# Two decay tiles for the S5 scan, gates' outputs in the input pool, other shares of matmuls between the parameters' steps

## The chip, the cores and the metric

One core of one Trainium2 chip runs the whole program in one launch. The metric is the time of an execution on the device in microseconds, as a median of several runs: 2692.31 us before the change (three runs, 2691.86 to 2693.35). The names of engines in the profile: PE is TensorE's matmuls and PEld its weight loads, DVE is VectorE, ACT is ScalarE, POOL is GpSimd, SP is the engine whose queue (SPq) issues the DMAs.

## The reference, cut to what matters

One encoder layer on x of 2048 tokens by 1024, float32:

```python
proj = rmsnorm(x, norm1_g) @ w_in
q, k, v, u, g_attn, g_ssm = split(proj)
attn = windowed_gqa(rope(q), rope(k), v, sink)          # |i-j| <= 128
ssm = bidirectional_s5(u, lam, log_dt, b, c, d, w_glu)  # 32 groups x 16 channels, 64 states, two directions
merged = sigmoid(g_attn) * (attn @ w_attn_branch) + sigmoid(g_ssm) * (ssm @ w_ssm_branch)
x = x + merged @ w_out
x = x + (silu(h2 @ w_ffn_gate) * (h2 @ w_ffn_up)) @ w_ffn_down   # h2 = rmsnorm(x)
y = rmsnorm(x)
```

In S5 each direction has the state recurrence h[t] = exp(lam dt) h[t-1] + Bbar u[t], and the output is Re(C (h_fwd + h_bwd)) + d u, then GELU and a gated linear unit.

## The kernel before, in words

Matmul operands are split into a high and a low float32r part and multiplied in three passes. All weights come through one pool of raw tiles, ScalarE or GpSimd writes the high part (lines 413, 415) and VectorE the low part (line 416). The gates' 32 column blocks (function `gates`) are matmuls at line 450: 48 for one block of 128 columns and one half of the tokens, evicted from the PSUM tag pj (two banks) by ScalarE's tanh at line 588 into a tile `go`, which a DMA stores to DRAM (gD). They depend on little, and serve as filling between other work.

The S5 parameters (`ssm_prep`) are computed in the first phase, under projections and gates of the first half of tokens. First come 32 tables of angles (tiles wt from products wn on GpSimd and wv on VectorE, lines 232 to 234, stored to cD), a yield after each fourth; then for eight batches of four groups the matrices E and F (tiles ef, products wm, same lines, on VectorE), a small tile bk (GpSimd: a memset at line 309, two copies at line 312, two buffers), a yield, and `ssm_turn`: TensorE transposes E (line 326) and multiplies bk with F (line 332), ScalarE and VectorE read the result (lines 334 to 341), DMAs store it (eD, tD). ef has four buffers, that is two batches. `ssm_prep` is a generator, and what it yields is a number of us: phase 1 then issues so many us of the main stream (a step of three matmuls at line 450 counts 0.681), and at the end the rest of it. TensorE's order there is the order of the program, written by hand. The other engines' order is fixed at build by a planner, which simulates the program and takes instructions by order of program, operands and free buffers.

Attention and the second half's projections follow, and then phase 2, the S5 scan over 16 pairs of groups (`ssm_pair`), again with TensorE's order by hand: for each pair X, 4.3 us of gates of the second half, the output matmuls (lines 398 to 400) of the pair two before, 4.3 us of gates. A pair runs so: TensorE makes X in PSUM (line 360), VectorE four products m with the angle tables (lines 365 to 368), GpSimd adds them to Y (lines 371, 372), ScalarE writes the decay tile A (line 376, two copies), VectorE runs the two scans, forward on one half of the partitions and backward on the other (lines 382, 383), reading A and Y and writing W; then four products n, in tiles of the same tag m (lines 385, 386, 388 on GpSimd, 387 on VectorE), their sums H (line 390 on GpSimd, 391 on VectorE), later TensorE's output matmuls and the GELU (lines 402 and 404 on ScalarE, 403 and 405 on VectorE). Behind this comes `branch_a_quarter`, attention's branch matmuls with operands `at`.

The input pool (`act`, tag a) has 20 tiles of 4 KB a partition; 16 hold the normalised input h of the second half in phase 2. In the scan's own pool m has six tiles, Y and W two, A one, and go two. What the change and the prediction touch: lines 248, 313, 364, 370, 384, 808.

Of the kernel before, what the change touches and what calls it, by code (L numbers as in the profile page):

```python
# [40 lines left out]
G0 = 3  # L41
# [24 lines left out]
def run(gen, us):  # L66

    while us > 0:
        c = next(gen, None)
        if c is None:  # L70
            break
        us -= c
    return us
# [13 lines left out]
def rest(gen):  # L87
    for _ in gen:
        pass


class Kern:
# [58 lines left out]
    def ssm_prep(self, pool, lam_re, lam_im, log_dt, b_re, b_im, c_re, c_im, d):  # L151
# [7 lines left out]
        W = lambda sh: pool.tile(sh, F32, tag="w", name="w")  # L159
# [70 lines left out]
        def outer(eng, fr, tag, a0, a1, op, dst, sh):  # L230
            m1, m2 = (fr.tile(sh, F32, tag=tag, name=tag) for _ in range(2))
            eng.tensor_tensor(m1, a0[0], a0[1], MULT)
            eng.tensor_tensor(m2, a1[0], a1[1], MULT)
            eng.tensor_tensor(dst, m1, m2, op)

        with ExitStack() as es:
            sub = self.pool("prept", 3, es)
            cc, cs = angles(sub, 17, 32, "t")
            sh2 = [128, 16, 16]
            lo = lambda z, g: z[:, g, 0:16].unsqueeze(1).to_broadcast(sh2)  # L240
            hi = lambda z, g: z[:, g, 16:32].unsqueeze(2).to_broadcast(sh2)
            for g in range(G):
                T = sub.tile([128, 2, 16, 16], F32, tag="wt", name="wt")
                e, tg = (p, "wn") if g % 2 == 0 else (v, "wv")
                outer(e, sub, tg, (lo(cc, g), hi(cc, g)), (lo(cs, g), hi(cs, g)), SUB, T[:, 0], sh2)
                outer(e, sub, tg, (lo(cc, g), hi(cs, g)), (lo(cs, g), hi(cc, g)), ADD, T[:, 1], sh2)
                if g % 4 == 3:
                    yield 14.5
                self.store(self.cD[:, g], T.rearrange("q r a b -> q r (a b)"))

        ce, se = angles(pool, 0, 17, "e")
# [44 lines left out]
        sh = [128, NG, 8, CH]  # L296
# [4 lines left out]
        for g0 in range(0, G, NG):  # L301
            E, F = (sub.tile([128, NG, 2, 8, CH], F32, tag="ef", name="ef", bufs=4) for _ in range(2))
            outer(v, sub, "wm", (ab(ewr, g0, 0), bb_(B[:, 0], g0)), (ab(ewi, g0, 0), bb_(B[:, 1], g0)), SUB, E[:, :, 0], sh)
            outer(v, sub, "wm", (ab(ewr, g0, 0), bb_(B[:, 1], g0)), (ab(ewi, g0, 0), bb_(B[:, 0], g0)), ADD, E[:, :, 1], sh)
            outer(v, sub, "wm", (ab(ce, g0, 8), bb_(C[:, 0], g0)), (ab(se, g0, 8), bb_(C[:, 1], g0)), SUB, F[:, :, 0], sh)
            outer(v, sub, "wm", (ab(ce, g0, 8), bb_(C[:, 1], g0)), (ab(se, g0, 8), bb_(C[:, 0], g0)), ADD, F[:, :, 1], sh)
            self.store(self.fD[:, g0:g0 + NG], F.rearrange("q g r t h -> q g r (t h)"))
            bk = sub.tile([128, 2, NG, 48], F32, tag="bk", name="bk", bufs=2)
            p.memset(bk, 0.0)
            for dd in range(2):  # L310
                q = slice(64 * dd, 64 * dd + 64)
                p.tensor_scalar(bk[q, :, :, 32 * dd:32 * dd + 16], bb[q, :, g0:g0 + NG], 1.0, 1.0, MULT, MULT)
            yield 8.5
            self.ssm_turn(pool, g0, NG, E, F, bk, dd_)
        es.close()

# [29 lines left out]
    def ssm_pair(self, pool, g0):  # L346

        nc, v, s, p, pe = self.nc, self.v, self.s, self.p, self.pe
        tl = lambda tag, sh, bufs: pool.tile(sh, F32, tag=tag, name=tag, bufs=bufs)
        E, U, cs = tl("E", [128, 2, 2, 128], 2), tl("U", [128, 2, NC], 4), tl("cs", [128, 2, 2, NC], 2)  # L350
        self.load(E, self.eD[:, g0:g0 + 2])
        for i in range(2):
            f0 = CH * (g0 + i)
            self.load(U[:, i], self.uD[:, f0:f0 + CH, :])
        self.load(cs, self.cD[:, g0:g0 + 2])
        X = []
        for r in range(2):
            x = self.ps("a" if r == 0 else "b", [128, 2, NC])
            for i in range(2):
                pe.matmul(x[:, i], E[:, i, r], U[:, i], start=True, stop=True)  # L360
            X.append(x)
        co, si = cs[:, :, 0], cs[:, :, 1]
        sh = [128, 2, NC]
        m = [tl("m", sh, 6) for _ in range(4)]
        v.tensor_tensor(m[0], X[0], co, MULT)
        v.tensor_tensor(m[1], X[1], si, MULT)
        v.tensor_tensor(m[2], X[1], co, MULT)
        v.tensor_tensor(m[3], X[0], si, MULT)
        sh2 = [128, 2, 2, NC]
        Y, W, a = tl("Y", sh2, 2), tl("W", sh2, 2), tl("A", sh2, 1)  # L370
        p.tensor_tensor(Y[:, 0], m[0], m[1], ADD)
        p.tensor_tensor(Y[:, 1], m[3], m[2], SUB)
        p.memset(Y[0:64, :, :, NC - 1:NC], 0.0)
        p.memset(Y[64:128, :, :, 0:1], 0.0)
        for i in range(2):
            s.activation(a[:, :, i], self.edge.unsqueeze(1).to_broadcast([128, 2, NC]), AF.Copy,
                         scale=self.r8[:, g0 + i:g0 + i + 1])
        Wf, Yf, af = (z.rearrange("q r g c -> q (r g c)") for z in (W, Y, a))
        n = 4 * NC
        p.memset(Wf[0:64, 0:1], 0.0)  # L380
        p.memset(Wf[64:128, n - 1:n], 0.0)
        v.tensor_tensor_scan(Wf[0:64, 1:n], af[0:64, 0:n - 1], Yf[0:64, 0:n - 1], 0.0, MULT, ADD)
        v.tensor_tensor_scan(Wf[64:128, n - 2::-1], af[64:128, n - 1:0:-1], Yf[64:128, n - 1:0:-1], 0.0, MULT, ADD)
        n = [tl("m", sh, 6) for _ in range(4)]
        p.tensor_tensor(n[0], W[:, 0], co, MULT)
        p.tensor_tensor(n[1], W[:, 1], si, MULT)
        v.tensor_tensor(n[2], W[:, 0], si, MULT)
        p.tensor_tensor(n[3], W[:, 1], co, MULT)
        H = [tl("H", sh, 4) for _ in range(2)]
        p.tensor_tensor(H[0], n[0], n[1], ADD)  # L390
        v.tensor_tensor(H[1], n[3], n[2], SUB)
        F, T = tl("F", [128, 2, 2, 128], 2), tl("T", [128, 2, 128], 2)
        self.load(F, self.fD[:, g0:g0 + 2])
        self.load(T, self.tD[:, g0:g0 + 2])
        yield
        y = self.ps("nt" if g0 % 4 else "c", sh)
        for i in range(2):
            pe.matmul(y[:, i], T[:, i], U[:, i], start=True, stop=False)
            pe.matmul(y[:, i], F[:, i, 0], H[0][:, i], start=False, stop=False)
            pe.matmul(y[:, i], F[:, i, 1], H[1][:, i], start=False, stop=True)  # L400
        g = tl("g", sh, 2)
        s.activation(g, y, AF.Square, scale=math.sqrt(0.044715))
        v.scalar_tensor_tensor(g, g, 1.0, y, ADD, MULT)
        s.activation(g, g, AF.Tanh, scale=0.7978845608028654)
        v.scalar_tensor_tensor(g, g, 1.0, y, ADD, MULT)
        for i in range(2):
            f0 = CH * (g0 + i)
            self.store(self.yD[f0:f0 + CH].rearrange("h t c -> t h c"), g[:, i])
# [387 lines left out]
    def phase2(self, w_in, w_ab):  # L796
        self.yD = self.dram.tile([512, L, NC], F32, name="yD")
        self.ma = {}
        self.mid_es = ExitStack()
        self.mid = self.pool("mid", 1, self.mid_es)  # L800
        self.hi_on_act = True
        with ExitStack() as es:
            pool = self.pool("p2", 1, es)
            self.edge = pool.tile([128, NC], F32, name="edge")
            self.p.memset(self.edge, 1.0)
            self.p.memset(self.edge[0:64, NC - 1:NC], 0.0)
            self.p.memset(self.edge[64:128, 0:1], 0.0)
            gt = self.gates(w_in, self.H1, 1, G0, 16, 1, pool, bufs=2)
            with self.tc.manual_schedule(engines={mybir.EngineType.PE}):
                due = run(gt, 15.0)  # L810
                P = [self.ssm_pair(pool, g) for g in range(0, G, 2)]
                for i in range(len(P) + 2):
                    if i < len(P):
                        next(P[i])
                    due = run(gt, due + 4.3)
                    if i > 1:
                        rest(P[i - 2])
                    due = run(gt, due + 4.3)
                rest(gt)
        W = self.branch_a_weights(w_ab)  # L820
        for q in range(4):
            self.branch_a_quarter(W, q)
# [460 lines left out]
```

## Time and profile before

| what | value |
|---|---|
| median of three runs | 2692.31 us |
| profiled execution, its own time | 2696.69 us |
| its span | 2694.9 us |
| mean granted TensorE clock | 0.978 |
| TensorE busy | 2566.2 us, 95% |
| VectorE busy | 1899.0 us, 70% |
| GpSimd busy | 1237.3 us, 46% |
| ScalarE busy | 1033.9 us, 38% |

The span runs from the first to the last instruction, the execution's own time also holds what lies around it. Busy shares are means over stages that differ; a row of the waits or of the timeline gives an engine's idle time before an instruction and, behind an arrow, what ended it. The granted clock is a share of 2.4 GHz, and 0.5 is 1.2 GHz.

### The profile page before, as it was taken

Reading aid. Unit: us, or ns where it says so; the run is one execution under the profiler, and the core shown is the slowest. Engines: PE = TensorE matmul, PEld = TensorE weight load, DVE = VectorE, ACT = ScalarE, POOL = GpSimd, SP = SyncE. Lnnn points to the kernel's source line nnn. Section 1 sums busy time; section 2 is a strip of 40 time slices with the busy share of each in tenths; the row PEclk is TensorE's granted clock in tenths of the full one; section 3 lists DMA queues with packets and bytes.
Section 4 is the critical chain, followed back from the end, with each engine's and each line's share of the span. In section 5 each row is a group of like instructions: output and inputs, shape, how many; then the busy total and the mean of one; then the engine's idle time right before and its main releaser. Section 6 shows DMA issues by size and latency. Waiting matters only on the chain.

```text
span 2694.9 us, 34635 instructions
## 1 busy us (share of the span) xinstructions
PE 2566.2 (95%) x12090; PEld 2124.8 (79%) x12090; DVE 1899.0 (70%) x2734; ACT 1033.9 (38%) x1878; POOL 1237.3 (46%) x1007
## 2 busy tenths in 40 slices
PE   8997999999999899999979999998999999999998
PEld 7886889988777678887758888877888887877887
DVE  5889477776677847656568888877777776466567
ACT  4222265676222213443454444444444445111113
POOL 2387122222455502215227667746656663354336
PEclk9998999999999899999989999999999999999999
DMA  5345542333554456666566565656455557676547
GB/s 163 105 142 196 162 151 77 93 83 107 179 165 150 144 138 197 199 201 211 190 203 184 172 180 156 187 178 202 141 155 145 161 150 240 253 282 238 222 181 261
DMA packets 451918, 467.95 MB, mean 174 GB/s; under 512 B 82848, under 2 KB 381856, under 8 KB 446624
## 3 DMA queue, kind: packets, MB, share of 16 engines
q1 hardware_dynamic: 451744, 465.75, 54.9%
q8 instruction: 95, 1.56, 0.2%
q14 instruction: 79, 0.65, 0.1%
HBM read 299.99 MB, written 165.68 MB: 173 GB/s over the span
## 4 chain that ended last, share of the span: by engine, by line
PE 42%; DVE 5%; DMA 3%; POOL 2%; issue 2%; ACT 1%; POOLq 0%; DVEq 0%; ACTq 0%; SPq 0%
PE ps_b L1003 17%; PE ps_pj L1003 11%; PE ps_a L1003 11%; DVE w L956 2%; PE ps_a L900 1%; PE ps_pj L450 1%; PE ps_b L900 1%; DMA hr<-h 1%; DMA hr<-h1S 1%; DVE zs L956 1%; DMA z<-z 1%; DVE H L956 1%; ACT H L955 0%; DMA raw<-in_w_ffn_up 0%; POOL T L974 0%
## 5 line engine op out<-in xcount | busy, mean ns | idle before, releaser
L450 PE MATMUL ps_pj<-h,w 128*128 128x512 f32 x1920 | 491.7, 406 | 21.9 <-ACT go L588 21.9
L450 PEld LDWEIGHTS ps_pj<-h,w 128*128 128x128 f32 x1920 | 358.5, 190 | 104.9 <-ACT go L588 25.2
L1003 PE MATMUL ps_b<-H,w 128*128 128x512 f32 x1584 | 384.4, 391 | 7.8 <-DVE u L1031 3.5
L1003 PEld LDWEIGHTS ps_b<-H,w 128*128 128x128 f32 x1584 | 297.9, 189 | 73.1 <-DVE u L1031 5.6
L1003 PE MATMUL ps_pj<-H,w 128*128 128x512 f32 x1056 | 268.1, 399 | 19.8 <-ACT c L1016 9.7
L1003 PE MATMUL ps_a<-H,w 128*128 128x512 f32 x1056 | 256.8, 391 | 0.0
L1003 PEld LDWEIGHTS ps_pj<-H,w 128*128 128x128 f32 x1056 | 202.3, 192 | 65.8 <-ACT c L1016 11.1
L956 DVE TENSOR_TENSOR w<-T,w 128x512 fp32r<-128x512 f32 x220 | 203.1, 927 | 70.0 <-ACT w L955 67.7
L956 DVE TENSOR_TENSOR w<-raw,w 128x512 fp32r<-128x512 f32 x165 | 198.5, 1205 | 49.7 <-ACT w L955 49.7
L1003 PEld LDWEIGHTS ps_a<-H,w 128*128 128x128 f32 x1056 | 199.1, 189 | 41.4
L955 ACT ACTIVATE w<-T 128x512 fp32r<-128x512 f32 x220 | 136.4, 626 | 223.0 <-PE ps_b L1003 69.6
L1003 PE MATMUL ps_b<-w,z 128*128 128x512 f32 x792 | 205.3, 395 | 5.9 <-DVE xa L1154 3.3
L416 DVE TENSOR_TENSOR w<-raw,w 128x1024 fp32r<-128x1024 f32 x111 | 149.8, 1350 | 72.4 <-ACT w L413 64.2
L1003 PEld LDWEIGHTS ps_b<-w,z 128*128 128x128 f32 x792 | 150.0, 190 | 40.3 <-DVE xa L1154 5.1
L413 ACT ACTIVATE w<-raw 128x1024 fp32r<-128x1024 f32 x93 | 98.0, 1055 | 158.5 <-PE ps_pj L450 84.8
L655 POOL TENSOR_SCALAR P<-P,st 128x384 f32<-128x384 f32 (+1 forms) x128 | 72.8, 588 | 186.8 <-DVE st L653 136.8
L460 PE MATMUL ps_pj<-w,h 128*128 128x256 f32 x1152 | 154.0, 285 | 4.2 <-DVE h L509 1.8
L974 POOL TENSOR_TENSOR T<-raw 128x512 f32<-128x512 f32 x55 | 84.4, 1534 | 157.1 <-DVE w L956 104.5
L460 PEld LDWEIGHTS ps_pj<-w,h 128*128 128x128 f32 x1152 | 142.4, 189 | 7.9 <-issue 2.0
L1154 DVE TENSOR_TENSOR xa<-xa,ps_b 128x512 f32<-128x512 f32 x128 | 87.3, 685 | 82.5 <-PE ps_b L1003 80.9
L955 ACT ACTIVATE w<-raw 128x512 fp32r<-128x512 f32 x165 | 102.9, 625 | 110.9 <-PE ps_pj L1003 32.8
L1003 PE MATMUL ps_a<-w,z 128*128 128x512 f32 x528 | 141.0, 392 | 3.3 <-DVE xa L1154 1.8
(332 smaller groups left out, 5038.6 us busy)
## 6 DMA issues: line engine op xcount, KB each, us to landing
z<-zs SPq DMA_DIRECT2D x308, 256.0 KB
z<-z SPq DMA_DIRECT2D x40, 1792.0 KB
raw<-in_w_in SPq DMA_DIRECT2D x52, 512.0 KB
raw<-in_w_ffn_gate SPq DMA_DIRECT2D x44, 512.0 KB
raw<-in_w_ffn_up SPq DMA_DIRECT2D x44, 512.0 KB
x<-in_x SPq DMA_DIRECT2D x32, 512.0 KB
gD<-go SPq DMA_DIRECT2D x32, 512.0 KB
tg<-gD SPq DMA_DIRECT2D x64, 256.0 KB
```

Of the source, the lines that this page charges most:

```text
L413: self.s.activation(hi, src, AF.Copy)
L416: (lo_eng or self.v).tensor_tensor(lo, src, hi.bitcast(F32), SUB)
L450: self.pe.matmul(ps, W[a][:, k, cs], H[k][:, b, sl], start=(i == 0), stop=(i == n - 1))
L460: self.pe.matmul(ps, H[k][:, a, off:off + 128], W[k // 4][b][:, k % 4, :], start=(i == 0), stop=(i == n - 1))
L655: p.tensor_scalar(P[i], P[i], den[:, i:i + 1], 1.0, MULT, MULT)
L900: self.pe.matmul(ps[t], M[k0 + k][:, a, 128 * t:128 * t + 128], W[b][:, k], start=(k0 + k + i == 0), stop=(k0 + k == 7 and i == 2))
L955: self.s.activation(hi, src, AF.Copy)
L956: self.v.tensor_tensor(lo, src, hi.bitcast(F32), SUB)
L974: eng.tensor_tensor(T[:, 0], b12, b11, SUB)
L1003: self.pe.matmul(ps, a, b, start=(first and i == 0), stop=(i == n - 1), skip_group_check=True)
L1154: v.tensor_tensor(x[n], x[n], ps, ADD)
```

## The change

Seven numbers and one call. Two yields of `ssm_prep` get other values. In `ssm_pair` the tag m has eight tiles and A two. In `phase2` the gates' outputs are allocated by the default of `gates`, which is the input pool, and no longer in two tiles of the scan's pool; the sizes of m and A take the place of these two tiles.

```diff
                 if g % 4 == 3:
-                    yield 14.5
+                    yield 17.3
                 self.store(self.cD[:, g], T.rearrange("q r a b -> q r (a b)"))
...
-            yield 8.5
+            yield 7.2
             self.ssm_turn(pool, g0, NG, E, F, bk, dd_)
...
-        m = [tl("m", sh, 6) for _ in range(4)]
+        m = [tl("m", sh, 8) for _ in range(4)]
...
-        Y, W, a = tl("Y", sh2, 2), tl("W", sh2, 2), tl("A", sh2, 1)
+        Y, W, a = tl("Y", sh2, 2), tl("W", sh2, 2), tl("A", sh2, 2)
...
-        n = [tl("m", sh, 6) for _ in range(4)]
+        n = [tl("m", sh, 8) for _ in range(4)]
...
-            gt = self.gates(w_in, self.H1, 1, G0, 16, 1, pool, bufs=2)
+            gt = self.gates(w_in, self.H1, 1, G0, 16)
```

## Rows read from the trace of the kernel before

**Rows 1.** The page's part 1: busy us, share of the span, instructions.
```profile
PE 2566.2 (95%) x12090; PEld 2124.8 (79%) x12090; DVE 1899.0 (70%) x2734; ACT 1033.9 (38%) x1878; POOL 1237.3 (46%) x1007
```

**Rows 2.** TensorE's waits: line, what it waited for, us in total, times, longest.
```profile
PE ps_pj L450 <- ACT go L588: 24.7, 9, 5.8
PE ps_nt L326 <- DVE ef L234: 14.5, 2, 14.3
...
PE ps_a L332 <- DVE ef L234: 2.5, 1, 2.5
```

**Rows 3.** Timeline of TensorE, parameters: start, us, line, count, idle before.
```profile
226.65 0.44 PE L326 MATMUL ps_nt<-cst,ef 128*128 128x128 f32 x1 [14.33 <-DVE ef L234]
...
235.19 9.94 PE L450 MATMUL ps_pj<-h,w 128*128 128x512 f32 x39
244.97 0.60 PE L326 MATMUL ps_nt<-cst,ef 128*128 128x128 f32 x4
...
267.66 0.60 PE L326 MATMUL ps_nt<-cst,ef 128*128 128x128 f32 x4
...
279.72 0.60 PE L326 MATMUL ps_nt<-cst,ef 128*128 128x128 f32 x4
...
317.29 24.07 PE L450 MATMUL ps_pj<-h,w 128*128 128x512 f32 x102
341.20 0.60 PE L630 MATMUL ps_b<-cst,q 128*128 128x128 f32 x4
```

**Rows 4.** Line 312 (ns, min/median/max), timelines of GpSimd and VectorE there.
```profile
L312 POOL TENSOR_SCALAR bk<-bb x16: 295/651/15011, 223.9 to 295.5; 64x128 f32<-64x128 f32 x16
...
235.89 11.96 POOL L312 TENSOR_SCALAR bk<-bb 64x128 f32<-64x128 f32 x2
...
248.51 15.71 POOL L312 TENSOR_SCALAR bk<-bb 64x128 f32<-64x128 f32 x2
...
268.74 1.29 DVE L234 TENSOR_TENSOR ef<-wm 128x512 f32<-128x512 f32 x2 [0.57 <-PE ps_c L326]
```

**Rows 5.** Windows: length, busy PE, PEld, DVE, ACT, POOL, clock, DMA, GB/s.
```profile
226.65:235.19 8.54, 5.85 (x24) 4.42 (x24) 8.54 (x14) 1.19 (x2) 0.06 (x1) 0.50 0.37 127
...
689.90:941.90 252.00, 224.64 (x924) 182.30 (x923) 192.82 (x174) 59.85 (x96) 143.74 (x156) 0.93 0.51 160
```

**Rows 6.** Timelines of the scan: first and second pair, one pair amid, the last.
```profile
696.49 2.28 DVE L382 TENSOR_TENSOR_SCAN W<-A,Y 64x1023 f32<-64x1023 f32 x1 [1.69 <-POOL Y L373]
...
704.57 0.68 DVE L366 TENSOR_TENSOR m<-ps_b,cs 128x512 f32<-128x512 f32 x1
...
793.15 1.81 POOL L385 TENSOR_TENSOR m<-W,cs 128x512 f32<-128x512 f32 x1 [4.56 <-DVE W L383]
793.16 1.34 ACT L376 ACTIVATE A<-edge,r 128x512 f32<-128x512 f32 x2 [10.88 <-DVE W L383]
...
797.38 1.28 POOL L390 TENSOR_TENSOR H<-m 128x512 f32<-128x512 f32 x1
...
800.55 1.30 POOL L371 TENSOR_TENSOR Y<-m 128x512 f32<-128x512 f32 x1 [1.71 <-DVE m L366]
...
929.47 2.27 DVE L382 TENSOR_TENSOR_SCAN W<-A,Y 64x1023 f32<-64x1023 f32 x1
```

**Rows 7.** VectorE's groups, 690 to 942 us: busy us, mean ns, idle before.
```profile
L391 DVE TENSOR_TENSOR H<-m 128x512 f32<-128x512 f32 x16 | 28.0, 1750 | 10.6 <-POOL m L388 10.6
L416 DVE TENSOR_TENSOR w<-raw,w 128x1024 fp32r<-128x1024 f32 x12 | 18.0, 1499 | 1.7 <-ACT w L413 1.6
L387 DVE TENSOR_TENSOR m<-W,cs 128x512 f32<-128x512 f32 x16 | 13.8, 865 | 0.5
```

**Rows 8.** Timeline of TensorE in the scan: two pairs' X, the last output.
```profile
866.79 1.03 PE L360 MATMUL ps_a<-U,E 128*128 128x256 f32 x4
...
880.19 1.03 PE L360 MATMUL ps_a<-U,E 128*128 128x256 f32 x4
...
939.71 0.70 PE L399 MATMUL ps_nt<-H,F 128*128 128x256 f32 x2 [0.61 <-POOL H L390]
```

## The prediction

> **What bounds the kernel now.** I read the page's busy times first: TensorE is busy for 2566.2 of 2694.9 us [rows 1], so 128.7 us of idle and what the lower clock costs are all there is to win without touching the matmuls. Then the waits of TensorE, longest first: two stand out [rows 2]. One is matmuls into ps_pj that wait until ScalarE has read the bank before (line 588, 24.7 us in 9 pieces), the other is a single wait of 14.3 us for the S5 parameters (line 326 for ef), with 2.5 us at line 332 behind it. The timeline of TensorE puts the second at 212.3 to 226.65 us [rows 3]. The first lies between 690 and 942 us, in the S5 scan [rows 5, 6]; there TensorE is busy for 224.6 of 252 us at a mean granted clock of 0.93 [rows 5]. The change aims at these two places, and they have different limits, so each has its own sum.
>
> **Parameters (the yields 17.3 and 7.2).** TensorE's order is written by hand: after each yielded number the main stream issues so many us of projections and gates. Eight yields of 14.5 become 17.3, so 8 x 2.8 = 22.4 us more of line 450 stand ahead of the first turn; eight of 8.5 become 7.2, so 8 x 1.3 = 10.4 us are taken from between the turns; the remaining 12 us come out of the tail behind the last turn, 24.07 us now [rows 3]. No matmul is added or removed.
> What is won: the first turn would come at 212.3 + 22.4 = 234.7 us, and E is there at 226.65, F about 5 us later, where the wait of 2.5 us ends. Two more weight splits get in front on VectorE (1.2 to 1.5 us each, [rows 7] has the dearer mean) and move F by some 3 us, to about 234.5; line 332 asks for it at 235.7. So 14.3 + 0.2 + 2.5 us of waiting go. The stretch behind the wait ran at 0.50 of the full clock [rows 5], 1.2 of 2.4 GHz: from 226.65 to 244.97 it took 18.3 us, less the 2.7 us of waits 15.6, where the same 39 gates matmuls and turn took 12.06 us later (267.66 to 279.72, [rows 3]). That is 3.6 us more. Sum 20.6 us.
> What is given back: turns will follow each other by 7.2 + 2.85 = 10.05 us (2.85 is the 12.06 less 9.2 for its 39 gates matmuls) instead of up to 12.06. VectorE gets E and F made ahead of that: at 268.74 it had to wait for a buffer of ef that a turn still read [rows 4]. GpSimd's bk is closer: its memset waits for the turn two before, and while VectorE ran without a gap two pairs of its copies (median 651 ns each) took 11.96 and 15.71 us [rows 4]. That wait at 268.74 was the first gap; with turns shifted later by 8 us but closer together that gap comes later or not at all. The window from a turn's last matmul to the next-but-one's line 332 is 18.2 us; bk of group 2 (from 237.6) ends at 250, that of group 3 at 266 against a need of 265.8. Cost between 0 (copies as the later ones) and 24 us (below); I take 2.5, near the lower end: the median is the nearest row, two pairs of eight were slow, and a late TensorE opens gaps in VectorE's queue. Behind the last turn 11.6 us are left before attention's first transpose instead of 23.9 [rows 3]; what must fit is the last tD stores and the first q loads, some 11 us: 0 to 3 us, I take 0.5. Net 17.6 us.
>
> **Scan (A, m, go).** ScalarE's decay copy (line 376) for the next pair waits 10.88 us for the second scan, because it writes the one tile that the scan reads [rows 6]; the evictions of gates queue behind it, both ps_pj banks are full, and TensorE stops. With two tiles that wait goes back one pair, and go in the input pool need not wait for the memory that attention leaves, which is worth little by itself, since the scan chain has not begun there. But TensorE stops because it is faster than the scan: the two scans of the first and of the last pair begin at 696.49 and 929.47, 15.53 us a pair [rows 6], while an undisturbed turn of TensorE takes 13.40 us (866.79 to 880.19, [rows 8]; 12.9 to 13.4 with 36 to 39 gates matmuls). At the end TensorE waits for the last pair itself: line 399 for H [rows 8]. So a wait removed at ScalarE only moves TensorE's idle time, unless the pairs follow each other faster. The gain is 15 times what a pair gets shorter.
> What shortens it is m: with six tiles the four n of a pair leave two for the next pair's m. Now GpSimd finishes H (797.38 + 1.28) and sits idle 1.71 us until VectorE, which does line 391 first, has made two of the next m [rows 6]. With eight tiles VectorE can make all four m while GpSimd makes n, and Y starts right behind H. Line 391 then falls between H and Y. Those two contend: line 391 takes 1750 ns each time where line 387, the same shape, has a mean of 865 ns and 690 when nothing is beside it [rows 7], because it stands still while line 390 runs. So 0.6 of the 1.71 comes back: 1.1 us a pair, 15 x 1.1 = 16 us. Bounds: 0, if VectorE's order, which the planner fixes at build, stays as now (m behind line 391, nothing shorter), and 15 x (15.53 - 13.1) = 36 us, if Y is made during the scan of the pair before and TensorE becomes the bound. Below zero I see only a VectorE order with more weight splits in the chain; 12 of them, 18 us, stand in it now [rows 7], so at most a few us. I take 16, near the middle, from the one idle that a row shows. Releasing go's two slots and giving them to A and m costs nothing in time; in the input pool four slots are free while the 16 tiles of h live, and branch A's at waits for the same ones, at the latest until the gates end, when sixteen come free. TensorE has H to wait for then anyway.
> The trace has GpSimd idle in every pair from Y to the end of the scans (4.56 us before line 385, [rows 6]), so no row shows a GpSimd operation beside a scan. The Trainium skill, "SBUF — State Buffer", section "SBUF: two separate sides", says that VectorE with two inputs in SBUF and a GpSimd operation that reads SBUF exclude each other for the whole instruction. Line 391 and the bk copies agree with it (1750 ns; 15.71 us). By that rule the scan, which reads A and Y, also shuts GpSimd out, and a pair can't fall under 2 x 2.28 + 6 x 1.28 + 2 x 0.69 + 18.0/16 = 14.7 us (durations from [rows 6, 7]), 12 us over the stage, for 2663 us in all; the 36 us would be out of reach.
>
> **The sum.** 17.6 + 16 = 33.6 us. The profiled execution took 2696.69 us (span 2694.9), 4.4 above the median of 2692.31; I take the difference over to the median: 2659 us.
>
> **Rivals.**
> Only the parameters gain. ScalarE still meets VectorE in each pair: the tanh at line 404 waits for line 403, which stands behind the scans, and go queues behind it; if the planner keeps m behind line 391 the pair stays at 15.5 us. For it: VectorE's order in the middle of the stage did not use the two m that are free now. Against it: in the second pair, before line 403 takes part, m stands ahead of line 391, at 704.57, while line 390 has not run [rows 6]. 2692.3 - 17.6 = 2675 us.
> TensorE becomes the bound in the scan. Y during the scan of the pair before, 13.1 us a pair: 17.6 + 36 = 54 us, 2638 us. For it: two A, two Y, two W and eight m allow it. Against: the two operations that exclude each other above.
> The rule of exclusion taken in full, as worked out: 2663 us; it lies inside the forecast's own range.
> Slower: bk starves. Place: line 332 of turns 3 to 7. If VectorE has no gap up to the last group, each bk takes 0.42 + 15.71 = 16.1 us against turns of 10.05: bk of group 7 ends at 250 + 5 x 16.1 = 330.5, asked for at 306, 24.5 us of waits. With the clock falling at three or four of them, 3.6 us each, some 37 us are lost against 20.6 gained: 2692 + 16 = 2709 us with nothing gained in the scan. It eats the whole gain of the stage from about 13 us a bk on and shows as slower from about 15. For it: the two pairs at 11.96 and 15.71. Against: a TensorE that is late makes VectorE wait for the bank at line 340, and that gap lets GpSimd in.
> The change does not do what it says: planner and slots move elsewhere and give back what is won, within 5 us of before.
>
> **Chances.** Forecast 0.45 (its own range 2650 to 2668); parameters alone 0.27 (2668 to 2682); TensorE bound 0.15 (2632 to 2650); nothing 0.07; slower by starving or by another order 0.06. Range 2637 to 2680: it holds the forecast, most of the second and half of the third. A measurement can tell 0.2%, about 5.4 us, from no change: faster 0.88, same 0.06, slower 0.06.
>
> **What would show it.** The wait for ef at line 326 gone and line 450 without a break to about 235 us; waits at line 332, if any, released by bk on GpSimd. In the scan: line 376 waiting far less for the scan than 10.88 us a pair; four m between lines 387 and 391; the first additions of Y right behind H; scans 14.4 us apart; line 399 or 400 still waiting for H at the end, some 33 us earlier. I am wrong if the scans stay 15.5 us apart, if they come 13 us apart, or if line 332 waits for more than 5 us.

## The result, and the profile after

The changed kernel takes 2679.26 us, median of four runs (2678.26 to 2682.68), against 2692.83 us for the kernel before beside it (2691.86 to 2695.62): a ratio of 0.995, interval 0.9938 to 0.9963, that is 13.6 us less. Forecast were 33.6 us less and 2659 us; the time lies at the upper edge of the range and nearest to the rival in which only the parameters gain (2675). The profiled execution took 2678.26 us, its span is 2676.5 us, the mean granted clock 0.984. Times are medians of runs in the usual state: one run of the second kernel with X early, 3245.07 us at a mean granted clock of 0.735, is left out below. The change itself is five numbers and one call: the two yields, the m count in two places, and the A count.

The page's part 1 after:

```profile
PE 2561.0 (96%) x12090; PEld 2120.7 (79%) x12090; DVE 1904.2 (71%) x2734; ACT 1033.4 (39%) x1878; POOL 1239.1 (46%) x1007
```

**Parameters.** TensorE's timeline in that stage, the lines that answer to [rows 3]:

```profile
224.77 10.89 PE L450 MATMUL ps_pj<-h,w 128*128 128x512 f32 x46
235.50 0.60 PE L326 MATMUL ps_nt<-cst,ef 128*128 128x128 f32 x4
...
236.47 1.95 PE L332 MATMUL ps_a<-ef,bk 128*48 128x128 f32 x16
238.34 7.96 PE L450 MATMUL ps_pj<-h,w 128*128 128x512 f32 x33
246.14 0.60 PE L326 MATMUL ps_nt<-cst,ef 128*128 128x128 f32 x4
...
311.39 11.46 PE L450 MATMUL ps_pj<-h,w 128*128 128x512 f32 x48
324.33 0.63 PE L630 MATMUL ps_b<-cst,q 128*128 128x128 f32 x4 [1.48 <-DMA x<-in_x]
```

No bracket stands at line 326: the 14.33 us of waiting are gone, and so are the 2.5 us at line 332. Attention's first transpose comes at 324.33 in place of 341.20 us, 16.9 us earlier. The eight turns follow each other by 10.44 us in the mean (the last one's line 326 is at 308.55 us). The windows view (its last four columns are granted clock, DMA share and GB/s) of the stretch that stood at 0.50 in [rows 5]:

```profile
226.65:235.19 8.54, 8.54 (x38) 6.90 (x37) 8.54 (x14) 0.57 (x2) 0.07 (x1) 1.00 0.39 130
```

GpSimd's bk, timeline (two copies in a row), and from the view of line 312 the line on who waited for it (us, times):

```profile
239.04 11.11 POOL L312 TENSOR_SCALAR bk<-bb 64x128 f32<-64x128 f32 x2
250.71 17.22 POOL L312 TENSOR_SCALAR bk<-bb 64x128 f32<-64x128 f32 x2
268.49 9.73 POOL L312 TENSOR_SCALAR bk<-bb 64x128 f32<-64x128 f32 x2
...
  PE ps_a L332: 0.5, 2
```

Three pairs of copies take over 9 us now, two did before [rows 4], and TensorE waited 0.5 us for them in all.

**Scan.** The view of line 382 (min, median and longest ns; first and last start) and a pair in the middle of the stage:

```profile
L382 DVE TENSOR_TENSOR_SCAN W<-A,Y x16: 2272/2281/2282, 683.2 to 916.1; 64x1023 f32<-64x1023 f32 x16
```

```profile
774.81 2.28 DVE L382 TENSOR_TENSOR_SCAN W<-A,Y 64x1023 f32<-64x1023 f32 x1 [1.70 <-POOL Y L373]
...
776.65 1.03 PE L360 MATMUL ps_b<-U,E 128*128 128x256 f32 x4
...
779.50 1.34 ACT L376 ACTIVATE A<-edge,r 128x512 f32<-128x512 f32 x2 [10.87 <-DVE W L383]
...
783.73 1.28 POOL L390 TENSOR_TENSOR H<-m 128x512 f32<-128x512 f32 x1
783.80 1.75 DVE L391 TENSOR_TENSOR H<-m 128x512 f32<-128x512 f32 x1 [0.38 <-POOL m L388]
...
785.48 0.68 DVE L365 TENSOR_TENSOR m<-ps_a,cs 128x512 f32<-128x512 f32 x1
...
786.90 1.30 POOL L371 TENSOR_TENSOR Y<-m 128x512 f32<-128x512 f32 x1 [1.71 <-DVE m L366]
```

From 683.16 to 916.12 us are 15 pairs of 15.53 us, as before [rows 6]. The reader is to see two things. Line 391 still stands ahead of line 365, and GpSimd still sits idle 1.71 us before Y, the very number of [rows 6]. X was in PSUM at 777.68, before the second scan ended (779.41), and line 365 shows no wait when its turn comes, so the trace shows nothing that kept the four m behind line 391 but VectorE's order. And the decay copy still waits 10.87 us.

Only at the start of the stage is the order the forecast one. VectorE's timeline there: line 391 of the first pair stands behind the second pair's m, line 391 of the third pair ahead of the fourth pair's:

```profile
692.45 0.68 DVE L368 TENSOR_TENSOR m<-ps_a,cs 128x512 f32<-128x512 f32 x1
693.18 1.76 DVE L391 TENSOR_TENSOR H<-m 128x512 f32<-128x512 f32 x1
...
720.87 1.74 DVE L391 TENSOR_TENSOR H<-m 128x512 f32<-128x512 f32 x1 [1.24 <-POOL m L388]
722.53 0.68 DVE L365 TENSOR_TENSOR m<-ps_a,cs 128x512 f32<-128x512 f32 x1
```

The waits from 640 to 931 us (in total, times, longest):

```profile
ACT A L376 <- DVE W L383: 136.1, 13, 12.1
...
POOL Y L371 <- DVE m L366: 32.6, 13, 8.6
...
PE ps_pj L450 <- ACT go L588: 22.2, 6, 6.4
```

With two A the copy at 779.50 is for the pair after next: two were written before the first scan, and each later one follows a scan. Its tile comes free with the same second scan as before, so the copy itself has gone one pair ahead and its wait with it. ScalarE stands as long as before, and TensorE's wait behind it is 22.2 us, 24.7 in [rows 2].

### The profile page after: what moved, and what is told of

Its sections match the earlier page's. It is cut to its first block, busy times and chain, and to the rows that moved or that the text cites. A ratio compares the mean times of both kernels' runs of the same rounds, so it can differ in the third digit from the quotient of the medians.

```text
span 2676.5 us, 34629 instructions
## 1 busy us (share of the span) xinstructions
PE 2561.0 (96%) x12090; PEld 2120.7 (79%) x12090; DVE 1904.2 (71%) x2734; ACT 1033.4 (39%) x1878; POOL 1239.1 (46%) x1007
## 4 chain that ended last, share of the span: by engine, by line
PE 70%; DVE 8%; POOL 8%; issue 5%; DMA 5%; ACT 2%; SPq 1%; POOLq 0%; DVEq 0%; ACTq 0%
PE ps_pj L450 17%; PE ps_b L1003 15%; PE ps_pj L1003 10%; PE ps_a L1003 10%; PE ps_pj L460 4%; PE ps_a L900 3%; PE ps_b L900 3%; DVE w L956 2%; PE ps_c L674 2%; PE ps_b L665 1%; POOL bk L312 1%; DMA raw<-in_w_ffn_up 1%; POOL m L385 1%; DVE zs L956 1%; PE ps_a L642 1%
## 5 line engine op out<-in xcount | busy, mean ns | idle before, releaser
L450 PE MATMUL ps_pj<-h,w 128*128 128x512 f32 x1920 | 490.9, 405 | 22.2 <-ACT go L588 22.2
```

The lines of the kernel that those rows point to most:

```text
L450: self.pe.matmul(ps, W[a][:, k, cs], H[k][:, b, sl], start=(i == 0), stop=(i == n - 1))
```

## The experiments

A pair is here a fifteenth of the time from the first to the last start of line 382 (383 in the kernel with Y early). Times are medians; each ratio is to the kernel before, beside it on the same chip.

| kernel | us | ratio, interval | pair, us |
|---|---|---|---|
| after | 2679.26 | 0.9950, 0.9938 to 0.9963 | 15.53 |
| yields only | 2676.39 | 0.9940, 0.9928 to 0.9952 | 15.53 |
| scan edits only | 2697.3 | 1.0021, 1.0011 to 1.0031 | 15.52 |
| yields and go | 2680.27 | 0.9953, 0.9938 to 0.9967 | 15.62 |
| after, X early | 2670.77 | 0.9925, 0.9911 to 0.9939 | 14.47 |
| the same again | 2670.07 | 0.9916, 0.9902 to 0.9931 | 14.45 |
| X early, six m | 2681.66 | 0.9959, 0.9947 to 0.9970 | 15.25 |
| before, yields and X early | 2678.22 | 0.9949, 0.9937 to 0.9962 | 15.15 |
| X early, one A, six U | 2670.76 | 0.9916, 0.9903 to 0.9929 | 14.43 |
| X, m and Y early | 2672.92 | 0.9925, 0.9913 to 0.9938 | 14.42 |
| X early, eight m, go as before | 2666.22 | 0.9904, 0.9891 to 0.9916 | 14.29 |

**The yields alone, and the scan's edits alone.** The first is the kernel before with 17.3 and 7.2, the second the kernel after with the old yields:

```diff
-                    yield 14.5
+                    yield 17.3
...
-            yield 8.5
+            yield 7.2
```

> The kernel before with the two yields of the changed one (17.3, 7.2) and nothing else. Theory A (the scan's pairs follow VectorE's order, which the edits of the scan left as it was, so the whole gain comes from the parameters): about 2677 us, all of the changed kernel's gain or up to 2 us more, no wait for ef at line 326, the scans of first and last pair 15.5 us apart in the mean. Theory B (the edits of the scan carry a part of the gain, and the parameters gave back more than thought): about 2684 us, half of the gain.

> The changed kernel with the old yields (14.5, 8.5): only eight m, two A and go in the input pool. Theory A: no gain, 2691 to 2695 us, scans 15.5 us a pair, line 376 still waiting some 11 us a pair for the second scan, the wait of 14 us at line 326 back. Theory B: some 2684 to 2688 us.

The yields alone give 14.7 us (2691.13 to 2676.39), all of the change's gain; their time is 2.9 us under the change's, which the two intervals do not separate. The scan's edits alone make the kernel 0.21% slower (2697.3 against 2691.13 us, interval 0.11 to 0.31%), which neither theory expected. So together they are a loss, and the question is which of them loses and why the pair does not get shorter.

**go in the input pool, without the other two.** The yields, and the call at line 808 as in the change; m has six tiles and A one.

> The yields and go in the input pool, but six m and one A as before. Theory A says that go in the input pool makes branch A's operands late (four splits, 3.8 us, in the chain of the last pairs) and costs 1 to 3 us against the yields alone: 2678 to 2680 us. Rival: go's place is worth nothing either way, as the yields alone.

2680.27 us, 3.9 above the yields alone; the intervals overlap, so this pair of runs by itself does not settle it. VectorE's timeline of this kernel shows a place where a cost can arise:

```profile
899.00 3.73 DVE L416 TENSOR_TENSOR at<-ar,at 128x512 fp32r<-128x512 f32 x4
902.66 2.27 DVE L382 TENSOR_TENSOR_SCAN W<-A,Y 64x1023 f32<-64x1023 f32 x1
```

go takes tiles that branch A's operands `at` had. With the yields alone the first four of their splits are made before the first scan (651.7 to 667.5 us); here they fall into the scan's chain, and that pair takes 17.7 us in place of 15.8, the next 15.4 in place of 16.0. The first matmul of line 900, which comes behind branch A's, is at 1049.2 us here and at 1046.1 with the yields alone. But 2.2 of these 3.1 us stand already at attention's first transpose (326.64 and 324.46 us), where go's place plays no part yet, so the two traces show some 1 us for it.

**X one pair earlier on TensorE.** This gives VectorE's order a reason to put the next m first. Beside the change's edits:

```diff
-        co, si = cs[:, :, 0], cs[:, :, 1]
+        yield; co, si = cs[:, :, 0], cs[:, :, 1]
...
+                next(P[0])
                 for i in range(len(P) + 2):
+                    if i + 1 < len(P):
+                        next(P[i + 1])
```

> The changed kernel with X of a pair issued one pair earlier on TensorE (before the m of the pair before), nothing else. VectorE's order then has the next pair's four m ahead of line 391, and from the sixth pair on the next pair's scans too. Theory A, scan limited by the order of VectorE and by GpSimd and VectorE excluding each other: 14.4 to 14.8 us a pair, 11 to 16 us less than the changed kernel, about 2666 us; line 371 no longer waits for line 366. If GpSimd can work beside the scans: about 13.1 us a pair and 2643 us. Rival, TensorE or ScalarE's queue limits the stage and not VectorE's order: no change from 2679 us.

Pairs of 14.47 us, 2670.77 us. VectorE and GpSimd amid the stage:

```profile
792.13 2.28 DVE L382 TENSOR_TENSOR_SCAN W<-A,Y 64x1023 f32<-64x1023 f32 x1 [1.32 <-POOL Y L373]
...
797.37 1.76 DVE L391 TENSOR_TENSOR H<-m 128x512 f32<-128x512 f32 x1
...
800.22 1.28 POOL L388 TENSOR_TENSOR m<-W,cs 128x512 f32<-128x512 f32 x1
801.46 1.31 POOL L390 TENSOR_TENSOR H<-m 128x512 f32<-128x512 f32 x1
...
803.03 1.30 POOL L371 TENSOR_TENSOR Y<-m 128x512 f32<-128x512 f32 x1
```

Line 391 at 797.37 runs before line 388 has made the last n of the pair scanned at 792.13, so it is that of the pair before. The four m of a pair, and from the sixth pair on its scans, now stand ahead of line 391 of the pair before. Y starts behind H, and the 32.6 us of waits before line 371 become 10.3. The shortening forecast for the pair is there, 15 x 1.06 = 16 us. But the time falls by only 8.5 us against the change (9.2 in the second run). Where the rest went, TensorE's timeline shows at the end of the stage, first of the kernel after, then of the second run with X early:

```profile
902.80 5.71 PE L450 MATMUL ps_pj<-at,w 128*128 128x512 f32 x23
...
917.15 0.79 PE L450 MATMUL ps_pj<-at,w 128*128 128x512 f32 x1
921.49 3.68 PE L450 MATMUL ps_pj<-at,w 128*128 128x512 f32 x9 [3.55 <-DVE ma L794]
...
925.25 3.85 PE L450 MATMUL ps_pj<-at,w 128*128 128x512 f32 x15
...
930.91 9.45 PE L450 MATMUL ps_pj<-at,w 128*128 128x512 f32 x39
```

```profile
899.65 5.01 PE L450 MATMUL ps_pj<-at,w 128*128 128x512 f32 x20
...
911.14 2.35 PE L450 MATMUL ps_pj<-at,w 128*128 128x512 f32 x6
...
913.56 0.58 PE L450 MATMUL ps_pj<-at,w 128*128 128x512 f32 x1
...
915.95 9.44 PE L450 MATMUL ps_pj<-at,w 128*128 128x512 f32 x39
```

The last output matmul of the scan ends near 930.91 and 915.95 us, where the last lines begin, 15.0 us apart. (The last scans start 18.4 us apart, 2.2 of them from an earlier first scan; some 3.5 go back behind the last scan, where with X early H of the pair before still has to be made.) But while TensorE waited for the last pairs it had done 48 of branch A's matmuls (23 + 1 + 9 + 15), and with shorter pairs 27 (20 + 6 + 1). The 21 others come later, at 9.45/39 = 0.242 us each 5.1 us. That leaves 9.9, and the first matmul of line 900 (903 with X early) is 9.8 us earlier (1047.6 and 1037.8 us):

```profile
L900 PE MATMUL ps_a<-w,m x384: 388/389/632, 1047.6 to 1341.6; 128*128 128x512 f32 x192
L903 PE MATMUL ps_a<-w,m x384: 388/389/796, 1037.8 to 1330.9; 128*128 128x512 f32 x192
```

**Which buffers matter then.** Four kernels, all with the new yields and X early: six m in place of eight; before's m, A and go; one A and six U; and the last with Y, too, ahead of the scans.

```diff
-        m = [tl("m", sh, 8) for _ in range(4)]
+        m = [tl("m", sh, 6) for _ in range(4)]
```

> The kernel after with X one pair ahead, but six m: two A and go in the input pool stay. Theory A (early X does it, the number of m hardly matters): within 2 us of the same with eight m, 2669 to 2673 us. Theory B (eight m are needed beside early X): pairs back at 15.2 us or more, 2677 to 2681 us.

> The kernel before with the new yields and with the matmuls into X of a pair placed one pair earlier on TensorE, nothing else: m 6, A 1, go where it was. Theory A (a pair is as long as GpSimd's chain n, H, Y behind the scans, and it gets shorter only where VectorE has made the first two m before GpSimd asks for Y; for that X must be there early, and six m do): pairs of 14.4 to 14.8 us and 2661 to 2668 us, some 4 us under the run with eight m, two A and go in the input pool, because go costs nothing here. Theory B (early X helps only with eight m and two A): pairs of 15.2 to 15.6 us, 2674 to 2678 us.

Six m take back most of the pair's gain, 15.25 and 15.15 us, and all of the time's, 2681.66 and 2678.22 us. Both lie by theory B (the times 0.7 and 0.2 us above its upper ends), and my theory that six m do is wrong. The second kernel's timelines of VectorE and of GpSimd show the missing tiles:

```profile
823.98 0.69 DVE L367 TENSOR_TENSOR m<-ps_b,cs 128x512 f32<-128x512 f32 x1 [2.29 <-POOL Y L371]
...
829.12 3.21 DVE L383 TENSOR_TENSOR_SCAN W<-A,Y 64x1023 f32<-64x1023 f32 x1
```

```profile
825.34 1.27 POOL L372 TENSOR_TENSOR Y<-m 128x512 f32<-128x512 f32 x1 [1.40 <-DVE m L368]
...
827.01 3.17 POOL L390 TENSOR_TENSOR H<-m 128x512 f32<-128x512 f32 x1
```

The third m waits until Y's first addition has freed two tiles, and the second addition waits 1.40 us for the fourth m. (H at 827.01 and the scan at 829.12 are both longer than alone; the run with H beside a scan, below, is about that.) So eight m and early X are needed together; the change has the one and not the other.

```diff
-        E, U, cs = tl("E", [128, 2, 2, 128], 2), tl("U", [128, 2, NC], 4), tl("cs", [128, 2, 2, NC], 2)
+        E, U, cs = tl("E", [128, 2, 2, 128], 2), tl("U", [128, 2, NC], 6), tl("cs", [128, 2, 2, NC], 2)
...
-        Y, W, a = tl("Y", sh2, 2), tl("W", sh2, 2), tl("A", sh2, 2)
+        Y, W, a = tl("Y", sh2, 2), tl("W", sh2, 2), tl("A", sh2, 1)
```

> The kernel after with X one pair ahead, one A in place of two, and six U in place of four, so that TensorE's 18.8 us of waits for the transfer of U go. Theory A (GpSimd's chain still sets the pair, TensorE's waits and ScalarE's decay tile lie beside it): the waits for U vanish, the wait of the decay copy comes back to 140 us or more, and the time moves by at most 3 us: 2668 to 2672 us. Theory B (with 14.5 us a pair TensorE is the bound, so its waits count): 2658 to 2664 us. Theory C (two A matter once X is ahead): 2674 us or more.

2670.76 us, theory A. The decay copy waits 128.1 us in place of 99.1 (140 or more were expected), and TensorE's 18.8 us of waits for the load of U are gone, with 19.1 us behind line 588 in their place; together they do not move the time. This run changes A and U at once, so by itself it leaves room for two effects that cancel. The last kernel below has one A and four U, its decay copy waits 98.7 us, and its pairs are the shortest: no run here shows a gain of two A.

**A GpSimd operation beside a scan.** Y of the next pair ahead of this pair's scans in the program, its memsets on VectorE (lines from 375 on are one further down):

```diff
-        p.memset(Y[0:64, :, :, NC - 1:NC], 0.0)
-        p.memset(Y[64:128, :, :, 0:1], 0.0)
+        v.memset(Y[0:64, :, :, NC - 1:NC], 0.0)
+        v.memset(Y[64:128, :, :, 0:1], 0.0)
+        yield
```

> The kernel after with X, m and Y of a pair placed ahead of the scans of the pair before, and Y's two edge memsets on VectorE in place of GpSimd: GpSimd then does Y of the next pair ahead of H of this one, and H falls beside the next pair's scan. Theory A (a scan, which reads A and Y, and a GpSimd addition that reads two tiles in SBUF exclude each other): H takes its 1.28 us plus what is left of the scan (up to 3.6 us), or the scan grows by 1.28 us, and pairs stay at 14.2 to 14.8 us, 2668 to 2673 us. Theory B (they run beside each other): H stays near 1.3 us and the scan at 2.28 us, pairs fall to about 14.0 us, where TensorE is the bound, 2661 to 2667 us.

Two stretches of its timeline:

```profile
720.69 1.26 POOL L391 TENSOR_TENSOR H<-m 128x512 f32<-128x512 f32 x1
720.70 3.39 DVE L383 TENSOR_TENSOR_SCAN W<-A,Y 64x1023 f32<-64x1023 f32 x1
724.12 2.29 DVE L384 TENSOR_TENSOR_SCAN W<-A,Y 64x1023 f32<-64x1023 f32 x1
...
853.04 2.28 DVE L383 TENSOR_TENSOR_SCAN W<-A,Y 64x1023 f32<-64x1023 f32 x1
853.14 3.28 POOL L391 TENSOR_TENSOR H<-m 128x512 f32<-128x512 f32 x1 [0.20 <-DVE Y L374]
...
855.36 3.21 DVE L384 TENSOR_TENSOR_SCAN W<-A,Y 64x1023 f32<-64x1023 f32 x1
```

Where H starts 0.01 us ahead, it takes 1.26 us and the scan 1.11 longer than alone (3.39 and 2.28). Where the scan starts ahead, it takes 2.28, H takes 3.28 (until 856.42, that is 1.10 behind the first scan's end), and the second scan in its turn 3.21. They exclude each other in both orders, theory A; pairs stay at 14.42 us, 2672.92 us.

**The best of it: early X, eight m, one A, go where it was.** The memory for m comes from F and g, one tile each:

```diff
-        F, T = tl("F", [128, 2, 2, 128], 2), tl("T", [128, 2, 128], 2)
+        F, T = tl("F", [128, 2, 2, 128], 1), tl("T", [128, 2, 128], 2)
...
-        g = tl("g", sh, 2)
+        g = tl("g", sh, 1)
```

> The kernel before with the new yields, the matmuls into X of a pair one pair earlier on TensorE and eight m, but with one A and with go where it was before; the memory for m comes from one F and one g in place of two. Theory A (early X and eight m together shorten the pair, two A do nothing, and go in the input pool costs some 4 us): pairs of 14.4 to 14.6 us as with the change's other buffers, no pair of 17 us, and 2664 to 2668 us, below every kernel so far. Theory B (go in the input pool costs nothing once the pairs are shorter): 2669 to 2673 us. Theory C (one F or one g is a new wait): pairs of 15 us or more, 2674 us or more.

> The kernel after with the matmuls into X of a pair one pair earlier, a second time, beside the run above on the same chip: 2668 to 2673 us by either theory; the difference to the run above is what go in the input pool costs when the pairs are short.

2666.22 and 2670.07 us, 3.9 us apart as with the long pairs (five runs each, 2664.91 to 2669.51 and 2667.15 to 2672.68). The kernels differ in one A, F and g as well as in go, so that it is go's place is likely and not shown alone. For it speaks the place: from the first matmul of line 360 to the first of line 903 the first takes 359.9 us and the second 365.0, and only in the second do four `at` splits stand ahead of the last scan, in a pair of 17.10 us; in the first they are made from 652.4 to 668.2. The view of line 382 for the first:

```profile
L382 DVE TENSOR_TENSOR_SCAN W<-A,Y x16: 2280/2280/2282, 682.0 to 896.4; 64x1023 f32<-64x1023 f32 x16
```

This kernel is 26.4 us faster than the one before beside it, nearly twice the change's 13.6.

## Why the prediction was wrong

**Parameters, 17.6 us: right within the interval.** The steps came nearly as told: line 450 without a break to 235.50 (234.7 forecast), both waits gone, the clock of the stretch at 1.00, E and F there in time. The turns are 10.44 us apart and not 10.05: a yield of 7.2 issues 30 or 33 matmuls, which take 7.3 to 8.0 us, and the first of the eight stands ahead of the first turn. That gave bk more time than the sum did. Taken back for bk were 2.5 us, measured 0.5; behind the last turn 0.5, measured 1.48 for a load. Attention begins 16.9 us earlier, and the yields alone give 14.7 us, by the interval 13 to 19.

**Scan, 16 us: wrong, and it is 16 of the 20 us of error.** The step that failed: "With eight tiles VectorE can make all four m while GpSimd makes n, and Y starts right behind H." It could, but its order is fixed at build, and only the first two intervals (14.38 and 14.33 us) have all four m ahead of line 391; from the third on (720.87 and 722.53 above) the order is that of before, and the 15 pairs take 15.53 us each in the mean, nothing less than before. I had written that bound down (0 us, m stays behind line 391) and set the rival on it at 0.27, because line 366 stood ahead of line 390 at 704.57 [rows 6]. That row was of a pair in which lines 403 and 405 take no part yet, the first pairs, not the steady ones; the middle pair in the same group showed the steady state, Y waiting 1.71 us for m. That the time still lies in the stated range is owed to its width, which took in the rival. Free buffers are a permission, and the order needed a cause: X early and eight m give it together (1.06 us a pair); eight m alone give nothing, X early alone 0.38 us.

**The size of that term was off as well.** "The gain is 15 times what a pair gets shorter" counts only the scan's chain. With pairs 1.06 us shorter the end of the stage came 15.0 us earlier and the kernel won 8.5 to 9.2, since TensorE's waits had been filled with 21 of branch A's matmuls that then come later. With the order as forecast, the sum would have been 17.6 + 9 and about 2666 us, an estimate from these numbers.

**A.** "With two tiles that wait goes back one pair", and so line 376 was to wait far less than 10.88 us a pair. That was wrong: the copy went ahead by a pair as well and still waits 10.87 us (155.2 us in 15 waits became 136.1 in 13). Right was that such a wait is worth little to the time: no run shows a gain of two A.

**go.** "costs nothing in time" is most likely wrong. The scan's edits together are a clear loss, and two pairs of kernels with go in one place and the other lie 3.9 us apart, but no run shows go's part alone clear of noise. I had counted who needs go's tiles and not who loses the input pool's.

**The rule of exclusion.** It was set as a rival inside the forecast's range; no row showed a scan beside GpSimd. The run with H beside a scan shows it, at 1.11 us for 1.26, and none of these kernels has pairs near the 13.1 us in the mean of the rival at 2638 us. The floor of 14.7 us worked out from it was 0.3 to 0.5 us too high as a mean from first to last scan: kernels with early X and eight m have 14.29 to 14.47. A part of that is one pair of 11.77 us (748.14 less 736.37 in the first run with X early), the one at which the scans first go ahead of line 391; the steady pairs behind it take 13.6 to 15.2. The Trainium skill, "SBUF — State Buffer", section "SBUF: two separate sides", says that whichever of the two starts first holds the shared port for its whole instruction; the rows at 720.69 and 853.04 agree, both ways round.

**Open.** Attention had moved by 16.9 us, the first matmul of line 360 moved by 15.5 (689.9 to 674.4) and the first scan by 13.3; what took the rest was not traced to an instruction. Nor is it settled which of the scan's edits makes their loss.

## What to carry to other kernels

Before a buffer is added, read from a pair in the steady part of the stage which instruction stands ahead of the one that is to come early; where the order is fixed at build, as here, a free tile changed nothing until that instruction's operand was also produced earlier in the program. A shorter chain beside a full engine is worth what is left after the filling that its gaps had held (here 15.0 us less 5.1). A tile moved to another pool can cost what the tiles there were for.

## What the runs showed of the hardware

VectorE's scans, on 64 partitions each, and a GpSimd addition did not run at the same time, whichever came first: 2.28 us become 3.39 beside an addition of 1.26 us, and an addition that meets a running scan takes 3.28 us. Short GpSimd copies under a VectorE without gaps (busy 17.30 of 17.30 us from 250.70) took 17.22 us for two, where a pair took 1.23 to 1.67 us later in the same stage, and yet cost TensorE only 0.5 us, because bk is made two turns ahead.
